# AdaLN columns and sums of output weights moved to earlier stages of an encoder block, gate transposes and a first pooling moved later

## The chip, the cores and the metric

One core of one Trainium2 chip runs the kernel. The metric is the device time of one execution in microseconds (us). TensorE (PE) multiplies matrices; VectorE (DVE), ScalarE (ACT) and GpSimd (POOL) do the rest, and SyncE (SP) issues most of the DMAs.

## What is computed

The reference is one encoder block, with B = 1, S = 2048 tokens, D = 1024, 4 mLSTM heads of 128, 4 pooling groups of 128 channels with windows 2, 4, 8 and 16, and a feed-forward width of 4096, all in float32:

```python
mod = silu(c) @ w_ada + b_ada
sh1, sc1, gt1, sh2, sc2, gt2 = split(mod, 6)
h = rmsnorm(x, g_mix) * (1 + sc1) + sh1
q, k, v, o, gates, u = split(h @ w_in, cuts)
hm = mlstm_scan(q, k, v, gates) + flip(mlstm_scan(flipped q, k, v, gates))
y_a = sigmoid(o) * rmsnorm_per_head(hm) * g_head
y_b = concat([(centred_mean(u_g, window_g) - u_g) @ w_pool[g] for g in groups]) * pool_scale
x = x + gt1 * (concat([y_a, y_b]) @ w_out)
h = rmsnorm(x, g_ffn) * (1 + sc2) + sh2
x = x + gt2 * (relu(h @ w_ff1) ** 2 @ w_ff2)
return rmsnorm(x, g_final)
```

## The kernel before

Every float32 operand of a large product is split into a high and a low part, and a product is three matmuls: high by high, low by high, high by low. For a weight, `wr` is the loaded tile (512 KB), `wh` its high part (a cast on ACT, line 395) and `wl` the low part (a subtraction on DVE, line 396). `Hh` and `Hl` are the parts of the normalised input, four blocks b of 512 tokens. `col_mm` multiplies one block by one column tile of a weight in 24 matmuls: `c15` to `c12` are the inputs u of pooling groups 3 to 0, `c4` to `c7` the heads' k and `c0` to `c3` their q.

The first 640 us consist of these stages. In the *v stage* (line 255 on) 16 token tiles of 128 run through 48 matmuls each, giving v and the gate columns; `vg_out` copies them and stores them to `vd`. In the *pooling stage* (line 415 on) groups g = 3, 2, 1, 0 each run four blocks of `col_mm(12 + g)`. After each block one step of the generator `gate_rows` (line 310) is taken: it makes the gates' running sums and maxima on DVE and ACT and transposes them on TensorE (`gT`, `gL`, `gM`, `gC`, `gD`). After block 1 the next weight is requested. After the last block of a group DVE makes the window sums s of u (lines 447 to 456), stores them to `yd`, and folds the group's output weight (`wor` scaled, a matmul `wof`, a copy `woe`, a store to `wod`). Then follow the ada columns of `MODS[g]` in `mod_col`: a load of 512 KB, a product with the activated c with its sum taken along (line 117), and an addition of the bias. Columns 16 to 23 make gt1.

After `qk_proj(0)`, which makes k and q of head 0, `scan` runs once for each head, 16 chunks of 128 tokens in both directions, with the next head's projections as filling. From head 1 on in the code, and in fact over the scans of heads 0 and 1, the generator `out_sums` (line 666) is stepped beside it: for four row tiles k it loads two rows of output weights (`os0_k` from the input, `os1_k` from `wod`), multiplies both by gt1, and stores to `wotd` three halves and four differences of halves, for the seven products of a Strassen-like output stage. Each head ends with transposes `hT` (line 632).

One pool tag, `raw`, gives all tiles `xs`, `ada`, `wr`, `wor` and `os` the same three buffers in turn. Outside the output and feed-forward stages, which are ordered by hand, a scheduler fixes the order of each engine's instructions ahead of the run; an instruction in `keep_in_program_order` is held in the order of the code. Each engine, and SP with its DMAs, then works through its list in that order. An instruction that waits holds up all that stand behind it on its engine.

## Time and profile before

| | us |
|---|---|
| median of three runs (lowest, highest) | 2042.19 (2037.84, 2043.9) |
| the profiled execution: device time | 2039.14 |
| its span in the trace | 2037.1 |
| TensorE busy, of the span | 1987.5 (98%) |
| VectorE busy | 1356.5 (67%) |
| ScalarE busy | 918.3 (45%) |

Times inside the profile count from the start of the span. A busy TensorE is not one at its peak, since matmuls overlap: a 512 column matmul is drawn with 0.39 us, but follows its forerunner by some 0.23 us. A wait is read from the bracket at the end of a timeline row: the idle time ahead of the instruction and what ended it. A granted clock (PEclk) of 1.00 is 2.4 GHz, 0.50 is 1.2 GHz.

### The profile page before, as it was taken

How to read it: one execution, taken by the hardware profiler on the slowest of the kernel's cores; microseconds unless marked ns; L12 is line 12 of the kernel's file. 1: busy time of each engine (PE TensorE's matmuls, PEld its weight loads, DVE VectorE, ACT ScalarE, POOL GpSimd, SP SyncE). 2: the span in 40 equal slices, each digit the busy share in tenths (PEclk: the TensorE clock that was granted, in tenths of full speed). 3: DMA queues.
4: the chain of work that ended last, by engine and by line, in shares of the span. 5: the costliest groups of instructions: out<-in, count | busy, mean ns of one | idle time of the engine just before them, and what ended most of it. 6: DMA issues, size and time to landing. Idle time of an engine off the chain costs nothing.

```text
span 2037.1 us, 27780 instructions
## 1 busy us (share of the span) xinstructions
PE 1987.5 (98%) x9591; PEld 1658.5 (81%) x9591; DVE 1356.5 (67%) x2456; ACT 918.3 (45%) x1704; POOL 129.7 (6%) x353
## 2 busy tenths in 40 slices
PE   7999999989999999999999999999999999999998
PEld 6997777778887888888888888888888888888886
DVE  6638636676646777555666766666877667768876
ACT  4721223333335668755556655556324224324432
POOL 1100012222210111000000000000000000000011
PEclk9999999999999999999999999999999999999999
DMA  8736867787548799765666766766887657648553
GB/s 339 237 108 209 285 205 220 253 254 226 180 131 271 236 270 315 209 196 182 224 203 224 228 226 215 226 206 225 280 268 257 225 156 262 224 158 275 187 165 132
DMA packets 298574, 452.87 MB, mean 222 GB/s; under 512 B 23569, under 2 KB 163137, under 8 KB 298306
## 3 DMA queue, kind: packets, MB, share of 16 engines
q1 hardware_dynamic: 228546, 413.35, 62.3%
q10 hardware_dynamic: 69888, 37.76, 6.1%
q8 instruction: 75, 1.23, 0.2%
q14 instruction: 65, 0.53, 0.1%
HBM read 290.40 MB, written 160.62 MB: 221 GB/s over the span
## 4 chain that ended last, share of the span: by engine, by line
PE 84%; DMA 7%; DVE 4%; issue 1%; ACT 1%; POOL 1%; SPq 1%; POOLq 0%; DVEq 0%; ACTq 0%
PE c L405 4%; PE c L404 4%; PE c L406 4%; DMA ua<-uad 1%; DMA ada<-in_w_ada 1%; DVE ada L117 1%; DMA wotd<-os 1%; DMA rob<-wotd 1%; DMA vraw<-in_w_v 1%; PE f000x L845 1%; PE o11x L845 1%; PE o10x L845 1%; PE o13x L845 1%; PE o03x L845 1%; PE o12x L845 1%
## 5 line engine op out<-in xcount | busy, mean ns | idle before, releaser
L404 PE MATMUL c<-Hh,wh 128*128 128x512 f32 x512 | 211.0, 412 | 0.0
L405 PE MATMUL c<-Hl,wh 128*128 128x512 f32 x512 | 203.4, 397 | 0.0
L406 PE MATMUL c<-Hh,wl 128*128 128x512 f32 x512 | 202.8, 396 | 0.5 <-DVE wl L396 0.5
L406 PEld LDWEIGHTS c<-Hh,wl 128*128 128x128 f32 x512 | 96.6, 189 | 20.5 <-DVE wl L396 0.9
L404 PEld LDWEIGHTS c<-Hh,wh 128*128 128x128 f32 x512 | 97.0, 189 | 17.3 <-issue 1.0
L405 PEld LDWEIGHTS c<-Hl,wh 128*128 128x128 f32 x512 | 97.1, 190 | 16.8 <-issue 0.7
L117 DVE SCALAR_TENSOR_TENSOR ada<-ada,c_bc 128x1024 f32<-128x1024 f32 x48 | 58.1, 1221 | 22.4 <-DMA ada<-in_w_ada 22.3
L581 ACT ACTIVATE ua<-ua,vcol 128x128 f32<-128x128 f32 x64 | 25.7, 401 | 103.2 <-POOL ua L577 103.1
L780 ACT CAST wb<-rwb 128x1024 fp32r<-128x1024 f32 x56 | 58.7, 1051 | 26.0 <-DMA rwb<-twd 25.8
L961 POOL TENSOR_TENSOR g300ss<-g300ss 128x1 f32<-128x1 f32 x2 | 0.9, 451 | 1079.9 <-ACT g300j L957 1079.9
L783 DVE TENSOR_TENSOR wb<-rwb,wb 128x1024 fp32r<-128x1024 f32 x56 | 68.3, 1219 | 0.8 <-ACT wb L780 0.7
L622 ACT ACTIVATE jk<-hm 128x128 bf16<-128x128 f32 x64 | 19.6, 307 | 83.0 <-DVE hm L620 82.3
L586 DVE TENSOR_TENSOR ua<-ua,q 128x256 f32<-128x256 f32 x64 | 26.4, 425 | 37.5 <-DMA ua<-uad 26.8
L577 POOL TENSOR_SCALAR_AFFINE_SELECT ua<-ua 128x128 f32<-128x128 f32 x64 | 26.6, 416 | 270.7 <-DMA ua<-uad 135.4
L625 DVE TENSOR_TENSOR hm<-hm,hss 128x256 f32<-128x256 f32 x32 | 14.7, 458 | 38.9 <-POOL hss L129 38.9
L255 PE MATMUL vgp<-vgh,Hh 128*128 128x272 f32 x128 | 38.2, 301 | 2.3 <-ACT Hh L208 2.3
L440 ACT COPY u<-c 128x512 f32<-128x512 f32 x16 | 9.4, 585 | 63.7 <-PE c L406 59.4
L783 DVE TENSOR_TENSOR ob<-rob,ob 128x1024 fp32r<-128x1024 f32 x14 | 17.1, 1224 | 30.5 <-ACT ob L780 29.9
L256 PE MATMUL v2p<-v2h,Hh 128*128 128x256 f32 x128 | 36.2, 286 | 1.1 <-ACT v2h L236 1.1
L257 PE MATMUL vgp<-vgl,Hh 128*128 128x272 f32 x128 | 37.2, 292 | 0.0
L259 PE MATMUL vgp<-vgh,Hl 128*128 128x272 f32 x128 | 37.0, 294 | 0.0
L585 DVE TENSOR_TENSOR ua<-ua,S 128x256 f32<-128x256 f32 x64 | 26.5, 413 | 14.9 <-PE S L584 14.7
(4048 smaller groups left out, 6071.3 us busy)
## 6 DMA issues: line engine op xcount, KB each, us to landing
rwb<-twd SPq DMA_DIRECT2D x56, 512.0 KB, 6.1
ada<-in_w_ada SPq DMA_DIRECT2D x48, 512.0 KB, 5.2
ua<-uad SPq DMA_DIRECT2D x64, 256.0 KB, 4.1
j<-in_w SPq DMA_DIRECT2D x32, 512.0 KB, 5.4
twd<-t SPq DMA_DIRECT2D x64, 256.0 KB, 3.0
twd<-j SPq DMA_DIRECT2D x48, 256.0 KB, 2.8
wr<-in_w_col SPq DMA_DIRECT2D x16, 512.0 KB, 4.9
q<-qkd SPq DMA_DIRECT2D x32, 256.0 KB, 3.6
```

What stands on the lines that cost most here:

```text
L117: ve.scalar_tensor_tensor(w, w, 1.0, c_bc, ALU.mult, ALU.mult, accum_out=mod[:, j:j + 1])
L255: pe.matmul(pa[:, :VG], hh, vgh[k], start=st, stop=False)
L256: pe.matmul(pb[:, :256], hh, v2h[k], start=st, stop=False)
L257: pe.matmul(pa[:, :VG], hh, vgl[k], start=False, stop=False)
L259: pe.matmul(pa[:, :VG], hl, vgh[k], start=False, stop=en)
L404: pe.matmul(ps, hh[:, k], Hh[b][:, k], start=k == 0, stop=False)
L405: pe.matmul(ps, hh[:, k], Hl[b][:, k], start=False, stop=False)
L406: pe.matmul(ps, hl[:, k], Hh[b][:, k], start=False, stop=k == KT - 1)
L577: gp.affine_select(W[:, 0], W[:, 0], pattern=[[1, P]], compare_op=ALU.is_ge, fill=NEG, base=0, channel_multiplier=-1)
L780: sc.copy(dst, src)
L783: ve.tensor_tensor(dst, src, asf(hi), ALU.subtract)
L845: pe.matmul(ps, a[:, k], b[:, k], start=start and k == 0 and n == 0, stop=k == 3 and n == 2, skip_group_check=not start)
```

## The change

Eighteen ada columns (16 to 33) move to the v stage, three after each of the tiles 8 to 13 (`VMODS`). The pooling groups keep 4 (g = 3), 6 (g = 2), 4 (g = 1) and 0 (g = 0) columns, where they had 10, 10, 8 and 4. `out_sums(k)` becomes a plain function that is called in the pooling stage, after (g, b) = (2, 2), (1, 0), (1, 2) and (0, 0), and it leaves the scans; gt1 for it comes from a transpose of columns 16 to 23 ahead of the groups. The folds of groups 3 and 2 stand behind group 3, those of 1 and 0 behind group 2. `gL` and `gC` stand one block later in the code and, like `gM`, are held there. The window sums of group 3 stand behind the first block of group 2.

```diff
@@ -28,7 +28,12 @@
 NEG = -1.0e30
 EVERY = 2
 
-MODS = (range(16, 20), range(20, 28), range(28, 38), range(38, 48))
+VMODS = {i: range(16 + 3 * (i - 8), 19 + 3 * (i - 8)) for i in range(8, 14)}
+MODS = ((), range(44, 48), range(38, 44), range(34, 38))
+
+
+FOLDS = ((), (), (1, 0), (3, 2))
+OSUMS = {(2, 2): 3, (1, 0): 2, (1, 2): 1, (0, 0): 0}
 VG = 272
 
 
@@ -298,6 +303,8 @@
                         for q in range(KT):
                             norm_later(b + 1, rb, xk, q)
                 vg_out(4 * b + j)
+                for n in VMODS.get(4 * b + j, ()):
+                    mod_col(n)
 
 
     gstack = ExitStack()
@@ -331,8 +338,9 @@
         ve.tensor_copy(lasts[fw, 1:2], m_[fw, P - 1:P])
         ve.tensor_copy(lasts[bw, 1:2], m_[bw, 0:1])
         yield
+        yield
         ps = tp("gL")
-        pe.transpose(ps[0:1, 0:P], lasts[:, 0:1], ident)
+        tc.keep_in_program_order(pe.transpose(ps[0:1, 0:P], lasts[:, 0:1], ident))
         pe.transpose(ps[0:1, P:2 * P], lasts[:, 1:2], ident)
         rows = pg.tile([1, 4, P], F32, name="g_rows")
         ve.tensor_copy(rows[:, 0:2, :], ps[0:1, 0:2 * P].rearrange("p (a n) -> p a n", a=2))
@@ -349,7 +357,7 @@
         ve.tensor_copy(r3[:, 1, :, 0:NT - 1], r2[:, 1, :, 1:NT])
         yield
         ps = tp("gM")
-        pe.transpose(ps[:, 0:1], rows[:, 3, :], ident[0:1, 0:1])
+        tc.keep_in_program_order(pe.transpose(ps[:, 0:1], rows[:, 3, :], ident[0:1, 0:1]))
         mp = gt("g_mp", 1)
         ve.tensor_copy(mp, ps[:, 0:1])
         ve.scalar_tensor_tensor(m_, b_, mp, m_, ALU.add, ALU.max)
@@ -372,8 +380,9 @@
         ve.tensor_copy(ul[fw], a[fw, P - 1:P])
         ve.tensor_copy(ul[bw], a[bw, 0:1])
         yield
+        yield
         ps = tp("gC")
-        pe.transpose(ps[:, 0:P], v, ident)
+        tc.keep_in_program_order(pe.transpose(ps[:, 0:P], v, ident))
         pe.transpose(ps[:, P:2 * P], wk, ident)
         pe.transpose(ps[:, 2 * P:3 * P], m_, ident)
         ve.tensor_copy(vcol, ps[:, 0:P])
@@ -411,6 +420,21 @@
     def mod_row(j0):
         return mod_d[j0:j0 + KT, :].rearrange("(o a) n -> o (a n)", o=1).broadcast_to([P, D])
 
+    def out_sums(k, gt1):
+
+        rows = [raw(f"os{h}_{k}") for h in range(2)]
+        for h, src in enumerate((w_o[k], wo_d[k])):
+            dma(rows[h], src)
+        for h in range(2):
+            ve.tensor_tensor(rows[h], rows[h], gt1, ALU.mult)
+        b11, b12, b21, b22 = [r[:, 512 * n:512 * n + 512] for r in rows for n in range(2)]
+        for place, b in ((0, b11), (1, b21), (5, b22)):
+            dma(wot_d[place, :, k], b)
+        for place, dst, x_, y_ in ((3, b11, b12, b11), (4, b12, b22, b12), (2, b22, b22, b11),
+                                   (6, b21, b21, b22)):
+            ve.tensor_tensor(dst, x_, y_, ALU.subtract)
+            dma(wot_d[place, :, k], dst)
+
 
     with tc.tile_pool(name="pu", bufs=2) as pu, tc.tile_pool(name="psU", bufs=2, space=PSUM) as psU:
         wpl = pu.tile([P, 4, P], F32, name="wpl", bufs=1)
@@ -420,10 +444,37 @@
         pgs = ExitStack()
         pg = pgs.enter_context(tc.tile_pool(name="pg", bufs=1))
         gates = gate_rows(pg)
-        w = col_weights(15)
-        for g in (3, 2, 1, 0):
+
+        def pooled(g, u, pinned):
+
             win = WIN[g]
             hw = win // 2
+            s = pu.tile([P, T + 16], F32, tag="s", name=f"s{g}", bufs=1)
+            n = T + 15
+            ins = ve.tensor_tensor(s[:, 0:n], u[:, 0:n], u[:, 1:n + 1], ALU.add)
+            if pinned:
+                tc.keep_in_program_order(ins)
+            d = 2
+            while d < win:
+                n -= d
+                ve.tensor_tensor(s[:, 0:n], s[:, 0:n], s[:, d:n + d], ALU.add)
+                d *= 2
+            s = s[:, 8 - hw:8 - hw + T]
+            ve.tensor_tensor(s[:, 0:8], s[:, 0:8], edgec[:, 16 * g:16 * g + 8], ALU.mult)
+            ve.tensor_tensor(s[:, T - 8:T], s[:, T - 8:T], edgec[:, 16 * g + 8:16 * g + 16], ALU.mult)
+            ve.scalar_tensor_tensor(s, s, 1.0 / win, u[:, 8:8 + T], ALU.mult, ALU.subtract)
+            for b in range(NB):
+                dma(y_d[b][:, 4 + g, :], s[:, 512 * b:512 * b + 512])
+
+        w = col_weights(15)
+        mt = tp("modT1")
+        pe.transpose(mt[0:KT, 0:P], mod[:, 16:16 + KT], ident)
+        me = evt("modT1e")
+        sc.copy(me[0:KT, 0:P], mt[0:KT, 0:P])
+        dma(mod_d[16:16 + KT, :], me[0:KT, 0:P])
+        gt1 = pu.tile([P, D], F32, name="gt1", bufs=1)
+        dma(gt1, mod_row(16))
+        for g in (3, 2, 1, 0):
             u = pu.tile([P, T + 16], F32, tag="u", name=f"u{g}")
             gp.memset(u[:, 0:8], 0.0)
             gp.memset(u[:, T + 8:T + 16], 0.0)
@@ -440,32 +491,26 @@
                 sc.copy(u[:, 8 + 512 * b:8 + 512 * b + 512], ps)
                 if b == 1:
                     wn = col_weights(11 + g if g else 4)
+                if (g, b) in OSUMS:
+                    out_sums(OSUMS[g, b], gt1)
+                if (g, b) == (2, 0):
+                    pooled(3, u3, True)
             w = wn
-
-            s = pu.tile([P, T + 16], F32, tag="s", name=f"s{g}", bufs=1)
-            n = T + 15
-            ve.tensor_tensor(s[:, 0:n], u[:, 0:n], u[:, 1:n + 1], ALU.add)
-            d = 2
-            while d < win:
-                n -= d
-                ve.tensor_tensor(s[:, 0:n], s[:, 0:n], s[:, d:n + d], ALU.add)
-                d *= 2
-            s = s[:, 8 - hw:8 - hw + T]
-            ve.tensor_tensor(s[:, 0:8], s[:, 0:8], edgec[:, 16 * g:16 * g + 8], ALU.mult)
-            ve.tensor_tensor(s[:, T - 8:T], s[:, T - 8:T], edgec[:, 16 * g + 8:16 * g + 16], ALU.mult)
-            ve.scalar_tensor_tensor(s, s, 1.0 / win, u[:, 8:8 + T], ALU.mult, ALU.subtract)
-            for b in range(NB):
-                dma(y_d[b][:, 4 + g, :], s[:, 512 * b:512 * b + 512])
-
-            wr = raw(f"wor{g}")
-            dma(wr, w_o[4 + g])
-            ve.tensor_scalar(wr, wr, pscale[:, g:g + 1], None, ALU.mult)
-            for n in range(2):
-                ps = psU.tile([P, 512], F32, tag="y", name=f"wof{g}_{n}")
-                pe.matmul(ps, wpl[:, g], wr[:, 512 * n:512 * n + 512], start=True, stop=True)
-                e = evt(f"woe{g}_{n}")[:, :512]
-                sc.copy(e, ps)
-                dma(wo_d[g][:, 512 * n:512 * n + 512], e)
+            if g == 3:
+                u3 = u
+            else:
+                pooled(g, u, False)
+
+            for f in FOLDS[g]:
+                wr = raw(f"wor{f}")
+                dma(wr, w_o[4 + f])
+                ve.tensor_scalar(wr, wr, pscale[:, f:f + 1], None, ALU.mult)
+                for n in range(2):
+                    ps = psU.tile([P, 512], F32, tag="y", name=f"wof{f}_{n}")
+                    pe.matmul(ps, wpl[:, f], wr[:, 512 * n:512 * n + 512], start=True, stop=True)
+                    e = evt(f"woe{f}_{n}")[:, :512]
+                    sc.copy(e, ps)
+                    dma(wo_d[f][:, 512 * n:512 * n + 512], e)
             for j in MODS[g]:
                 mod_col(j)
         pgs.close()
@@ -663,26 +708,6 @@
                 sc.copy(e, ps)
                 dma_act(o_d[b][:, h, :], e)
 
-        def out_sums(gt1):
-
-            for k in range(4):
-                rows = [raw(f"os{h}_{k}") for h in range(2)]
-                for h, src in enumerate((w_o[k], wo_d[k])):
-                    dma(rows[h], src)
-                yield
-                for h in range(2):
-                    ve.tensor_tensor(rows[h], rows[h], gt1, ALU.mult)
-                    yield
-                b11, b12, b21, b22 = [r[:, 512 * n:512 * n + 512] for r in rows for n in range(2)]
-                for place, b in ((0, b11), (1, b21), (5, b22)):
-                    dma(wot_d[place, :, k], b)
-                yield
-                for place, dst, x_, y_ in ((3, b11, b12, b11), (4, b12, b22, b12), (2, b22, b22, b11),
-                                           (6, b21, b21, b22)):
-                    ve.tensor_tensor(dst, x_, y_, ALU.subtract)
-                    yield
-                    dma(wot_d[place, :, k], dst)
-
         def chain(*gs):
             for g in gs:
                 yield from g
@@ -695,9 +720,6 @@
         me = evt("modTe")
         sc.copy(me[0:48, 0:P], mt[0:48, 0:P])
         dma(mod_d, me[0:48, 0:P])
-        gt1 = wp.tile([P, D], F32, tag="bc", name="gt1", bufs=1)
-        dma(gt1, mod_row(16))
-        osum = out_sums(gt1)
         for h in range(H):
             Cn = [None] * NT
             if h + 1 < H:
@@ -709,8 +731,6 @@
                 n += 1
                 if n % EVERY == 0:
                     next(fill, None)
-                if h > 0 and n % 4 == 0:
-                    next(osum, None)
             for _ in fill:
                 pass
             Cb = Cn
```

What this does to the engines' order is shown at three places. The names: `vd3` is the store of block 3's v, `vt13` the tile it is from, `xs15` a token tile of x.

SP at the end of v, before:

```order
L189 DMA xs15_1045<-in_x 128x1024
L392 DMA wr15_1577<-in_w_col 128x1024
L392 DMA wr14_1661<-in_w_col 128x1024
L271 DMA vd2_129<-vt8_1158 128x4x129
L461 DMA wor3_1766<-in_w_o 128x1024
```

SP in the last tiles of v, in the changed kernel:

```order
L276 DMA vd3_130<-vt13_1498 128x4x129
L126 DMA ada31_1503<-in_w_ada 128x1024
L126 DMA ada32_1507<-in_w_ada 128x1024
L126 DMA ada33_1511<-in_w_ada 128x1024
L401 DMA wr15_1649<-in_w_col 128x1024
L276 DMA vd3_130<-vt14_1566 128x4x129
L401 DMA wr14_1740<-in_w_col 128x1024
```

The load of c15's weight, `wr15`, stood behind the last token tile, some six tiles of v ahead of its use; it stands behind `ada33` and the store of tile 13's v now.

VectorE at the low part of c12's weight, before; s1 are group 1's window sums, `u1` its input:

```order
L396 TENSOR_TENSOR wl12_2066<-wr12_2063,wh12_2065 128x1024
L462 TENSOR_SCALAR wor1_2131<-wor1_2131,pscale_241 128x1024
L447 TENSOR_TENSOR s1_2121<-u1_2008 128x2063
L117 SCALAR_TENSOR_TENSOR ada20_2144,mod_90<-ada20_2144,c_bc_87 128x1024
L451 TENSOR_TENSOR s1_2121<-s1_2121 128x2061
```

VectorE at the same place in the changed kernel; `os0_2` and `os1_2` are the two rows of `out_sums(2)`:

```order
L122 SCALAR_TENSOR_TENSOR ada43_2086,mod_90<-ada43_2086,c_bc_87 128x1024
L454 TENSOR_TENSOR s1_2237<-u1_2090 128x2063
L128 TENSOR_TENSOR mod_90<-mod_90,bada_200 128x1
L429 TENSOR_TENSOR os0_2_2119<-os0_2_2119,gt1_1660 128x1024
L429 TENSOR_TENSOR os1_2_2120<-os1_2_2120,gt1_1660 128x1024
L460 TENSOR_TENSOR s1_2237<-s1_2237 128x2061
L435 TENSOR_TENSOR os0_2_2119<-os0_2_2119 128x512
L405 TENSOR_TENSOR wl12_2165<-wr12_2162,wh12_2164 128x1024
```

`wl12` stood ahead of the first sum over u1; it stands behind two sums, two products with gt1 and one subtraction now.

VectorE at the low part of c4's weight, before; s0 and `u0` belong to group 0:

```order
L117 SCALAR_TENSOR_TENSOR ada27_2172,mod_90<-ada27_2172,c_bc_87 128x1024
L123 TENSOR_TENSOR mod_90<-mod_90,bada_200 128x1
L396 TENSOR_TENSOR wl4_2234<-wr4_2231,wh4_2233 128x1024
L462 TENSOR_SCALAR wor0_2298<-wor0_2298,pscale_241 128x1024
L117 SCALAR_TENSOR_TENSOR ada16_2311,mod_90<-ada16_2311,c_bc_87 128x1024
L447 TENSOR_TENSOR s0_2289<-u0_2176 128x2063
```

VectorE at the same place in the changed kernel:

```order
L454 TENSOR_TENSOR s0_2393<-u0_2263 128x2063
L128 TENSOR_TENSOR mod_90<-mod_90,bada_200 128x1
L122 SCALAR_TENSOR_TENSOR ada47_2259,mod_90<-ada47_2259,c_bc_87 128x1024
L429 TENSOR_TENSOR os0_0_2292<-os0_0_2292,gt1_1660 128x1024
L128 TENSOR_TENSOR mod_90<-mod_90,bada_200 128x1
L429 TENSOR_TENSOR os1_0_2293<-os1_0_2293,gt1_1660 128x1024
L463 TENSOR_TENSOR s0_2393<-s0_2393,edgec_1644 128x8
L464 TENSOR_TENSOR s0_2393<-s0_2393,edgec_1644 128x8
L465 SCALAR_TENSOR_TENSOR s0_2393<-s0_2393,u0_2263 128x2048
L435 TENSOR_TENSOR os0_0_2292<-os0_0_2292 128x512
L405 TENSOR_TENSOR wl4_2338<-wr4_2335,wh4_2337 128x1024
```

`wl4` stood ahead of the first sum over u0; it stands behind all of s0, one ada column and the products of `out_sums(0)` now.

## Rows read from the trace of the kernel before

**Rows 1.** Part 4 of the page: shares of the chain that ended last.

```profile
PE 84%; DMA 7%; DVE 4%; issue 1%; ACT 1%; POOL 1%; SPq 1%; POOLq 0%; DVEq 0%; ACTq 0%
```

**Rows 2.** Waits of PE: line, waited for; us in total, times, longest.

```profile
PE gL L335 <- issue: 4.1, 1, 4.1
...
PE kvb L508 <- DMA wr<-in_w_col: 1.0, 1, 1.0
```

**Rows 3.** Windows: stretch; us busy (and count) per engine, PEclk, DMA share, GB/s.

```profile
110.00:120.00 10.00, 10.00 (x85) 10.00 (x85) 1.08 (x4) 0.75 (x2) 0.10 (x1) 1.00 0.19 54
155.60:159.00 3.40, 3.36 (x10) 2.67 (x10) 3.37 (x13) 0.00 (x0) 0.00 (x0) 0.50 0.27 54
```

**Rows 4.** Timeline of PE at gL: start us, us, instruction [idle before <-releaser].

```profile
155.34 0.27 PE L335 MATMUL gL<-ident,g_last 128*1 128x128 f32 x1 [4.06 <-issue]
```

**Rows 5.** Groups of instructions, 134 to 256 us: busy us, mean ns | idle before.

```profile
L117 DVE SCALAR_TENSOR_TENSOR ada<-ada,c_bc 128x1024 f32<-128x1024 f32 x32 | 38.9, 1221 | 16.8 <-DMA ada<-in_w_ada 16.7
...
L447 DVE TENSOR_TENSOR s<-u 128x2063 f32<-128x2063 f32 x4 | 9.2, 2303 | 0.2 <-ACT u L440 0.2
L456 DVE SCALAR_TENSOR_TENSOR s<-s,u 128x2048 f32<-128x2048 f32 x4 | 9.1, 2286 | 0.0
...
L396 DVE TENSOR_TENSOR wl<-wr,wh 128x1024 fp32r<-128x1024 f32 x5 | 6.1, 1224 | 5.9 <-ACT wh L395 5.9
L395 ACT CAST wh<-wr 128x1024 fp32r<-128x1024 f32 x5 | 5.3, 1051 | 13.0 <-DMA wr<-in_w_col 11.2 <-PE v2p L260 1.9
```

**Rows 6.** The tile os: ns min/median/max, first and last start.

```profile
L674 DVE TENSOR_TENSOR os<-os,gt x8: 1212/1226/1226, 302.6 to 436.1; 128x1024 f32<-128x1024 f32 x8
L682 DVE TENSOR_TENSOR os<-os x8: 681/691/692, 307.6 to 446.0; 128x512 f32<-128x512 f32 x8
```

**Rows 7.** DMA issues, 134 to 256 us: KB each, median us to landing.

```profile
ada<-in_w_ada SPq DMA_DIRECT2D x32, 512.0 KB, 4.3
...
wr<-in_w_col SPq DMA_DIRECT2D x6, 512.0 KB, 4.7
```

**Rows 8.** Timeline of DVE in the last tiles of v.

```profile
123.12 0.42 DVE L269 COPY vt<-v2p 128x256 f32<-128x256 f32 x1
...
132.77 1.23 DVE L396 TENSOR_TENSOR wl<-wr,wh 128x1024 fp32r<-128x1024 f32 x1 [3.41 <-ACT wh L395]
```

**Rows 9.** Timelines of ACT and then of PE at c12.

```profile
211.15 0.59 ACT L440 COPY u<-c 128x512 f32<-128x512 f32 x1 [0.41 <-PE c L406]
...
212.05 0.50 PE L406 MATMUL c<-Hh,wl 128*128 128x512 f32 x1 [0.47 <-DVE wl L396]
212.71 1.13 PE L465 MATMUL wof<-wor,wpl 128*128 128x512 f32 x2 [0.17 <-DVE wor L462]
```

**Rows 10.** Timeline of PE at the first c4 matmuls.

```profile
235.73 0.39 PE L404 MATMUL c<-Hh,wh 128*128 128x512 f32 x1
235.95 0.39 PE L405 MATMUL c<-Hl,wh 128*128 128x512 f32 x1
237.12 1.98 PE L465 MATMUL wof<-wor,wpl 128*128 128x512 f32 x4 [0.78 <-DVE wor L462]
```

**Rows 11.** Timeline of PE: first and last hT of heads 0 and 2, last of head 1.

```profile
308.11 0.27 PE L632 MATMUL hT<-ident,hm 128*128 128x128 f32 x1
...
372.13 0.30 PE L632 MATMUL hT<-ident,hm 128*128 128x128 f32 x1 [0.84 <-DVE hm L625]
...
454.11 0.30 PE L632 MATMUL hT<-ident,hm 128*128 128x128 f32 x1 [0.96 <-DVE hm L625]
...
471.17 0.27 PE L632 MATMUL hT<-ident,hm 128*128 128x128 f32 x1
...
529.42 0.30 PE L632 MATMUL hT<-ident,hm 128*128 128x128 f32 x1 [0.85 <-DVE hm L625]
```

**Rows 12.** Timelines of DVE and of PE in the scan of head 1.

```profile
394.84 1.23 DVE L674 TENSOR_TENSOR os<-os,gt 128x1024 f32<-128x1024 f32 x1 [1.28 <-DMA os<-in_w_o]
...
396.38 0.49 PE L597 MATMUL n<-Cf,ua 128*128 128x129 f32 x2 [1.47 <-DVE Cf L607]
```

## The prediction

> **What bounds the kernel now.** I read the page first, then the waits of TensorE, then the stretches in which it waits, instruction by instruction. The chain of work that ended last is TensorE for 84% of the span [rows 1], so only what TensorE waits for is worth anything. From the output stage on (about 640 us to the end) it hardly waits, and the change does not reach there. It acts on four stretches of the first 460 us: the last tiles of v, the pooling stage (134 to 236 us), the first block of k, and the scans of heads 0 and 1. In the pooling stage the largest wait is gL, 4.1 us [rows 2]; after it the granted clock is 0.50 for 3.4 us, the 1.2 GHz level [rows 3, 4]. The waits at c12 and at wof0 are 0.5 and 0.8 us [rows 9, 10]. In the middle of v, VectorE has work for 1.08 of 10 us [rows 3]. In the scans VectorE holds TensorE up whenever an out_sums operation stands before the carried state Cf: at 394.84 it waits 1.28 us for os, works 1.23 us, and TensorE loses 1.47 us [rows 12].
>
> The sum is made against the profiled execution, 2039.14 us (span 2037.1). The median of the three runs, 2042.19, is 3.05 us above it; I take the difference as it comes out and put it on the median.
>
> **The change, part by part.**
>
> *v stage.* Eighteen ada columns cost VectorE 18 x 1.22 = 22 us [rows 5]; between tiles 8 and 15 it has that time, and TensorE does not wait for the columns. So the operations cost nothing while v lasts. Their loads are the price: SP issues wr15 only behind ada33, and its buffer is freed by ada31's product. Tile 13's copies end at about 123.5 [rows 8]; its store is issued, then ada31's load, at 123.9. Loads take 4.3 (ada) and 4.7 us (wr) in this stretch [rows 7]: ada31 at 128.2, its product 129.5, wr15 at 134.2, the cast of 1.05 and the subtraction of 1.22 us [rows 5] at 136.5. TensorE wants wl15 at 134.9, and in the kernel before it was done at 134.0 [rows 8]. **Cost +1.6** (0 to 3).
>
> The Trainium skill, page "DMA: Bandwidth & Descriptors", section on the anatomy of one DMA, fits 2.0 us plus the bytes over 436 GB/s, on another issue path than SP's; for 512 KB an estimate of 3.2 us. The rows are longer, 4.3 and 4.7. By the page's price wr15 would come 2.6 us earlier and the sum of all terms would be about 3 us lower, since c4 below also hangs on loads in a row.
>
> *Gate transposes.* gL stands after the whole of group 3 (near 158 us) instead of inside it. Its input was ready at 155.3 [rows 4], VectorE has fewer ada columns in front, so the wait of 4.1 and the half-clock stretch after it (3.4 us at half rate, 1.7 lost [rows 3]) both go: **-5.8**. What is late next is wof1, ahead of c13: its weight's scaling stands on VectorE behind the whole of group 3's pooling, which now begins after c14_0 (about 167.6). That is five wide operations of 2.2 to 2.3 us, three subtractions of 0.6, the small gate work and the scaling, some 17.5 us, while TensorE has 16.4 us of matmuls. **+1.3** (0 to 3); the other gate transposes have a block each and wait for nothing new.
>
> *c12, the last group's weights.* Before, wl12 was computed ahead of group 1's pooling and TensorE waited 0.47 us for it, and 0.17 for wof1 [rows 9]. Now it stands on VectorE behind the first add of s1, two products with gt1, the second add and one subtraction. The first add needs the whole of u1, that is the copy of c13's last block, and TensorE has nothing left then but four matmuls of c12 (0.9 us at 0.23 each [rows 10]). From the copy's start: 0.59 + 2.2 + 1.2 + 1.2 + 2.2 + 0.6 + 1.2 = 9.2 us [rows 5, 6, 9], with start-up 9.4, less 0.9: **+8.5**, less the 0.6 of before. This is a floor of the written order; loads can only lengthen it (wr12 waits for ada43's product, whose load waits behind the stores of s2). Range 7.9 to 11.
>
> *c4, the first k weights.* The same again: wl4 stands behind the first add of s0 (it needs c12's last block), ada47's product, two products with gt1, the edge products, the final step of s0 and one subtraction: 0.6 + 2.2 + 1.3 + 2.4 + 0.3 + 2.2 + 0.6 + 1.2 = 10.8, less four matmuls: floor 9.9. Here loads come close as well: ada44 to ada47 are issued behind the stores of out_sums(1), then the two rows of out_sums(0) and wr4 each behind a product, three loads of 4.3 to 4.7 us in a row. I take **+11** (9.6 to 14), nearer to the floor since only one of the chains has to be late for more; less the 0.8 of wof0's wait, which goes [rows 10].
>
> *The clock.* The waits at c12 and c4 are both longer than the one that was followed by 3.4 us at 0.50 [rows 3, 4], so each is charged **+1.7** (0 to 1.8).
>
> *out_sums leaves the scans.* Eight products of 1.23 and sixteen subtractions of 0.69, eight of which are in the row [rows 6], are 21 us of VectorE; what counts is the length of a head. From the last hT of head 0 to that of head 1 is 82.0 us, from there to that of head 2, which has no such work, 75.3: **-6.7**. Within head 0 the hT span 64.0 us, within head 2 58.25: **-5.8** [rows 11]. Together -12.5 (10 to 14; the heads have the same matmuls, but head 0's start is not aligned).
>
> *First block of k.* kvb waited 1.0 us [rows 2]; with TensorE 18 us later the loads there have landed: **-1** (-2.5 to +1).
>
> Sum: 1.6 - 5.8 + 1.3 + (8.5 - 0.6 + 1.7) + (11 - 0.8 + 1.7) = +18.6 up to k; -12.5 - 1 after it: **+5.1 us**. The profiled execution would take 2044.2, the median 2047.
>
> **The rivals.**
>
> *Faster: the moved work meets idle engines.* If wl15 and wof1 come in time, both waits are at their floors and no clock falls, the stage costs -5.8 + (7.9 - 0.6) + (9.6 - 0.8) = +10.3; with the best of the scans and of k (-14, -2.5) the change gains 6.2 us: 2036. For it: VectorE is idle in v and held TensorE up in the scans [rows 3, 12]. Against it: the floors follow from the order of one engine, and a wait of 4.1 us did lower the clock. The Trainium skill, page "Perfetto Trace Analysis", section Optimization Strategy, says that a kernel whose most contended engine changes over time may gain by interleaving these stretches; by that rule the change ends here. No run shows it yet. Chance 0.12, of which 0.11 lies beyond the bound named below.
>
> *Slower: the SP queue decides.* SP issues in program order, and now 28 stores and 8 loads of out_sums stand there among the ada loads. If ada47's load lands after about 247 us (some 5 us instead of 4.3 for each of the three before it), wr4 is issued later than VectorE's own chain allows, c4 waits 14 instead of 11; the same at c12 makes 11 out of 8.5, and wof1 3 out of 1.3. That is +3 + 2.5 + 1.7 = +7.2 on the forecast, +12.3 in all: 2054.5. For it: landings in the tuned stretch are already 4.3 to 4.7 [rows 7], and the stage gains traffic. A seventh of this price already passes the upper bound. Chance 0.37.
>
> *The change doesn't do what it says.* gL's input could be late even after c15_3, if the four ada columns of group 3 hold VectorE as before; then 2 to 4 us of the 5.8 come back: 2050. The transposes have 11 us more than before, so this has 0.04, counted among the slower ones.
>
> **How the numbers follow.** A measurement here can tell 0.3%, 6.1 us, from no change: below 2036.1 is faster, above 2048.3 slower. The forecast of 2047 lies inside, close to the upper bound; it has the rest, 0.47, and the terms' ranges around it (about 4 us either way, taken as independent) put 0.03 of this above the bound. So faster is 0.11; same 0.44 and the 0.01 of the gainful rival that stays inside, 0.45; slower 0.37, 0.04 and 0.03, 0.44. The forecast's own range is 2043 to 2051; the range that should hold the time 8 times in 10 reaches to most of both rivals, 2039 to 2057.
>
> **What would show it.** In the profile of the changed kernel: no wait at gL and a granted clock of 1.00 from 150 to 160 us; a wait of TensorE for wl of 8 us or more at c12 (near 212 us) and of 10 or more at c4 (near 245), each with matmuls at half rate behind it; no os operations after 302 us, and the last hT of heads 0, 1 and 2 some 75 us apart. If the waits at c12 and c4 are a few us only, the order on VectorE is not what binds there and the kernel is faster; if the heads stay 82 us apart, something other than out_sums sets their length and it is slower by far.

## The result and the profile after

The changed kernel takes 2053.0 us (median of four runs, 2051.45 to 2054.18) and the kernel before 2041.79 beside it: a ratio of 1.0060, 95% interval 1.0047 to 1.0073. It is slower by 0.6%, some 12 us. The two profiled executions, 2054.17 and 2039.14, lie 15.0 us apart, at spans of 2052.4 and 2037.1; the traces are compared on that pair, and about 3 us of their distance are a matter of which executions were profiled.

In the changed kernel TensorE is busy for 1991.9 us, 97% of the span. The shares of the chain that ended last ([rows 1] of before):

```profile
PE 86%; DMA 6%; DVE 5%; ACT 1%; issue 1%; POOL 0%; SPq 0%; DVEq 0%; POOLq 0%; ACTq 0%
```

The largest waits of TensorE in the changed kernel, with total, times and longest in us ([rows 2] of before):

```profile
PE c L413 <- ACT wh L404: 22.0, 3, 10.1
```

The wait for gL is gone. In its place stand three waits for the high part of a weight, `wh`, which is cast once the tile has landed, one for a scaled output weight, `wor`, and one for a low part, `wl`. The timeline of TensorE shows where: c15, wof1, c12 (twice) and c4.

```profile
142.93 0.79 PE L413 MATMUL c<-Hh,wh 128*128 128x512 f32 x1 [6.68 <-ACT wh L404]
...
198.08 2.93 PE L510 MATMUL wof<-wor,wpl 128*128 128x512 f32 x3 [3.73 <-DVE wor L507]
...
230.17 0.79 PE L413 MATMUL c<-Hh,wh 128*128 128x512 f32 x1 [5.22 <-ACT wh L404]
...
234.32 0.80 PE L415 MATMUL c<-Hh,wl 128*128 128x512 f32 x1 [2.08 <-DVE wl L405]
...
267.64 0.79 PE L413 MATMUL c<-Hh,wh 128*128 128x512 f32 x1 [10.06 <-ACT wh L404]
```

The four stretches behind these waits, in the view of [rows 3]:

```profile
142.93:146.30 3.37, 3.33 (x7) 2.22 (x8) 2.92 (x5) 1.46 (x3) 0.00 (x0) 0.50 0.91 293
...
198.00:201.40 3.40, 3.32 (x5) 1.51 (x5) 1.38 (x4) 0.58 (x1) 0.00 (x0) 0.53 1.04 382
...
230.00:238.70 8.70, 6.45 (x14) 4.67 (x15) 8.43 (x10) 0.12 (x1) 0.00 (x0) 0.50 0.69 207
267.60:272.80 5.20, 5.05 (x11) 3.56 (x12) 4.15 (x6) 0.00 (x0) 0.00 (x0) 0.50 0.80 299
```

The matmuls there are drawn with 0.63 instead of 0.39 us, the granted clock is 1.2 GHz. At half rate 3.33, 3.32, 6.45 and 5.05 us of work lost about 1.7, 1.6, 3.2 and 2.5 us.

The transposes hT, as in [rows 11]: the first of head 0, then the last of heads 0, 1 and 2.

```profile
336.57 0.27 PE L677 MATMUL hT<-ident,hm 128*128 128x128 f32 x1
...
394.65 0.30 PE L677 MATMUL hT<-ident,hm 128*128 128x128 f32 x1 [0.85 <-DVE hm L670]
...
470.37 0.30 PE L677 MATMUL hT<-ident,hm 128*128 128x128 f32 x1 [0.91 <-DVE hm L670]
...
544.35 0.30 PE L677 MATMUL hT<-ident,hm 128*128 128x128 f32 x1 [0.85 <-DVE hm L670]
```

The scans start 28.5 us later than before (336.57 against 308.11) and give 13.5 us back: head 0 spans 58.1 us instead of 64.0, head 1 75.7 instead of 82.0, head 2 74.0 instead of 75.3. After them nothing changes: the last matmul starts 15.2 us later than before.

**Why c15 waits.** VectorE, then SP, then ACT at the end of v:

```profile
127.93 1.23 DVE L122 SCALAR_TENSOR_TENSOR ada<-ada,c_bc 128x1024 f32<-128x1024 f32 x1 [1.57 <-DMA ada<-in_w_ada]
...
129.38 0.42 DVE L274 COPY vt<-v2p 128x256 f32<-128x256 f32 x1
...
135.93 1.23 DVE L122 SCALAR_TENSOR_TENSOR ada<-ada,c_bc 128x1024 f32<-128x1024 f32 x1 [3.46 <-DMA ada<-in_w_ada]
...
130.07 0.38 SPq L276 DMA_DIRECT2D vd<-vt  x1
130.50 2.14 SPq L126 DMA_DIRECT2D ada<-in_w_ada  x3
137.20 0.33 SPq L401 DMA_DIRECT2D wr<-in_w_col  x1
...
141.83 1.04 ACT L404 CAST wh<-wr 128x1024 fp32r<-128x1024 f32 x1 [4.02 <-DMA wr<-in_w_col]
```

The last matmul of tile 13 starts at 123.89, but VectorE works in order and waits for an ada load until 127.93; only after that product is the copy of the tile's v made, at 129.38. SP holds the store of that copy ahead of the next three ada loads, so they go out at 130.50. wr15 waits for the product of the first of them, which waits for its load until 135.93, and is issued at 137.20; TensorE has no weight until 142.93. VectorE waits for an ada load, and SP behind it for VectorE's copy. In the last four tiles with columns the longest of VectorE's waits were 1.8, 3.4, 1.6 and 3.5 us.

**Why c4 and c12 wait.** VectorE, SP and ACT ahead of c4:

```profile
253.16 1.23 DVE L122 SCALAR_TENSOR_TENSOR ada<-ada,c_bc 128x1024 f32<-128x1024 f32 x1 [1.60 <-DMA ada<-in_w_ada]
...
257.20 1.23 DVE L122 SCALAR_TENSOR_TENSOR ada<-ada,c_bc 128x1024 f32<-128x1024 f32 x1 [2.62 <-DMA ada<-in_w_ada]
...
259.69 2.30 DVE L454 TENSOR_TENSOR s<-u 128x2063 f32<-128x2063 f32 x1
...
261.98 1.22 DVE L122 SCALAR_TENSOR_TENSOR ada<-ada,c_bc 128x1024 f32<-128x1024 f32 x1
...
268.55 1.22 DVE L405 TENSOR_TENSOR wl<-wr,wh 128x1024 fp32r<-128x1024 f32 x1
...
263.23 0.33 SPq L401 DMA_DIRECT2D wr<-in_w_col  x1
...
266.54 1.04 ACT L404 CAST wh<-wr 128x1024 fp32r<-128x1024 f32 x1 [8.35 <-DMA wr<-in_w_col]
```

wr4 takes the buffer that ada47's product (261.98) sets free. That product stands behind three others, two of which wait for their loads (1.60 and 2.62 us), and behind the first add of s0 (259.69). TensorE ends c12 at 257.6 and stands until 267.64. c12 has the same form: ada41 to ada43 keep the three raw buffers, the first of their products waits 5.7 us for its load, and wr12 is issued only at 224.47; its cast starts at 229.08.

The loads are one half of it. The other half is VectorE's list, shown here at c12 (ACT's copy of the last block of u1 first):

```profile
224.99 0.58 ACT L491 COPY u<-c 128x512 f32<-128x512 f32 x1 [4.85 <-PE c L415]
...
225.67 2.31 DVE L454 TENSOR_TENSOR s<-u 128x2063 f32<-128x2063 f32 x1 [1.23 <-issue]
...
233.05 1.22 DVE L405 TENSOR_TENSOR wl<-wr,wh 128x1024 fp32r<-128x1024 f32 x1
```

From the first add of s1 to the end of wl12, 234.27, VectorE works without a gap. TensorE gets wh12 at 230.17, runs the four matmuls that need no wl, and waits again, until 234.32. At c4 wl4 ends at 269.77 and TensorE goes on with it at 269.82. So with this order on VectorE an earlier wr12 or wr4 alone would have gained next to nothing (an estimate from these rows).

### The profile page after: what moved, and what is told of

It is laid out like the page before. It is cut to its first block, busy times and chain, and to the rows that moved or that the text cites. A ratio compares the mean times of both kernels' runs of the same rounds, so it can differ in the third digit from the quotient of the medians.

```text
span 2052.4 us, 27805 instructions
## 1 busy us (share of the span) xinstructions
PE 1991.9 (97%) x9592; PEld 1663.4 (81%) x9592; DVE 1363.1 (66%) x2456; ACT 919.7 (45%) x1705; POOL 128.0 (6%) x353
## 4 chain that ended last, share of the span: by engine, by line
PE 86%; DMA 6%; DVE 5%; ACT 1%; issue 1%; POOL 0%; SPq 0%; DVEq 0%; POOLq 0%; ACTq 0%
PE c L415 5%; PE c L414 5%; PE c L413 5%; DMA ada<-in_w_ada 2%; DVE ada L122 1%; PE S L629 1%; PE n L640 1%; PE kvf L647 1%; PE n L643 1%; DVE xk L224 1%; PE n L645 1%; PE n L642 1%; DMA vraw<-in_w_v 1%; DMA ua<-uad 1%; PE f000x L865 1%
```

## The experiments

Two readings were to be told apart. By the first, each wait is the price of one moved part and goes with it. By the second, the waits hang together through the raw buffers and SP's list, so that a wait taken away at one place comes back at the next. The diffs are against the changed kernel unless said otherwise; where one shows only lines with a +, these take the place of the changed kernel's.

**The sums back in the scans.**

```diff
-                if (g, b) in OSUMS:
-                    out_sums(OSUMS[g, b], gt1)
...
+                if h > 0 and n % 4 == 0:
+                    next(osum, None)
```

> The changed kernel with out_sums back in the scans (columns in v, folds, gates and the late first pooling stay). Theory A, waits for weights: in the changed kernel the loss sits in four waits of TensorE, for c15's weight (6.9 us), for wof1's scaled weight (3.7), for c12's (5.4 + 2.2) and for c4's (10.2), because the loads of ada columns, output rows and weights take turns in three buffers and one queue; without out_sums there, the last three go (under 1 us each) and the scans of heads 0 and 1 get their 12.5 us back: against the kernel before +1.6 for the end of v, +8.6 for c15's wait with its half-clock stretch, -5.8 for gL, -1 for waits of before that go: +3 us (0 to 6). Theory B, amount of work: the stage is full of VectorE work and traffic, whatever their order; then the columns alone cost as well, two of the three waits stay in part, and it is +10 or more against before. Last hT of heads 0 and 1: 82 us apart by both.

Measured 2035.5 us, ratio 0.9971 (0.9960 to 0.9981): faster than before, where a loss of 3 was expected. The wait at c15 stays (5.4 us), those at wof1, c12 and c4 go, and the first k transposes come at 249.1 us, 3 later than before and 29 earlier than in the changed kernel. The forecast held up to there; then the way from there to the last hT of head 3 took 6.5 us less than before, 3.9 of them up to the first hT, which the sum didn't hold. Moving the sums into the pooling stage thus costs 0.9%, 18 us, net of the 12 that the scans gain.

**Fifteen columns in v instead of eighteen**, the other three in group 3.

```diff
-VMODS = {i: range(16 + 3 * (i - 8), 19 + 3 * (i - 8)) for i in range(8, 14)}
-MODS = ((), range(44, 48), range(38, 44), range(34, 38))
+VMODS = {i: range(16 + 3 * (i - 8), 19 + 3 * (i - 8)) for i in range(8, 13)}
+MODS = ((), range(44, 48), range(38, 44), range(31, 38))
```

> The changed kernel with the three columns of tile 13 (31 to 33) taken back to group 3. Theory A: the load of c15's weight stands behind one turn less of the three buffers; the wait of 6.9 us at the start of the pooling stage falls to under 1.5 and its half-clock stretch (1.7) goes, while the other waits stay: 7 us (5 to 9) less than the changed kernel, so +4 against before. Theory B: three more columns in the pooling stage cost what they save, it stays at +11 (+8 to +13).

Measured 2055.54, 1.0077 (1.0062 to 1.0092): no gain. TensorE's timeline at c12 and c4:

```profile
229.88 0.79 PE L413 MATMUL c<-Hh,wh 128*128 128x512 f32 x1 [11.81 <-ACT wh L404]
...
265.58 0.80 PE L413 MATMUL c<-Hh,wh 128*128 128x512 f32 x1 [11.85 <-ACT wh L404]
```

The wait at c15 fell from 6.7 to 1.4 us, as expected, but c12 starts at 229.88 instead of 230.17 and only waits longer for it. The loads and products ahead of wr12 set that time, and what is saved ahead of them is worth nothing: the second reading.

**Only the gate transposes**, on the kernel before; the third transpose, gC, likewise.

```diff
         yield
+        yield
         ps = tp("gL")
-        pe.transpose(ps[0:1, 0:P], lasts[:, 0:1], ident)
+        tc.keep_in_program_order(pe.transpose(ps[0:1, 0:P], lasts[:, 0:1], ident))
...
-        pe.transpose(ps[:, 0:1], rows[:, 3, :], ident[0:1, 0:1])
+        tc.keep_in_program_order(pe.transpose(ps[:, 0:1], rows[:, 3, :], ident[0:1, 0:1]))
```

> The kernel before with the later gate transposes alone (gL and gC one block later, the three held in their places); columns, out_sums, folds and first pooling as before. Theory A: the wait of 4.1 us at gL and the 1.7 us of its half-clock stretch go and nothing takes their place: -5.8 us (-7 to -4). Rival: group 3's window sums stand on VectorE between gL and gM, so the wait moves to gM or gC and at most 2 us are gained.

Measured 2039.93, 1.0001 (0.9991 to 1.0011). TensorE first, then VectorE:

```profile
171.46 0.23 PE L353 MATMUL gM<-ident,g_rows 1*128 1x1 f32 x1 [3.99 <-DVE g_rows L350]
...
168.84 2.27 DVE L453 TENSOR_TENSOR s<-s 128x2061 f32<-128x2061 f32 x1
171.04 0.17 DVE L349 COPY g_rows<-g_rows 1x60 f32<-1x60 f32 x1
```

The 4.1 us of gL come back as 4.0 us at gM, whose input stands behind group 3's window sums on VectorE.

**The sums in the scans, without the two further `yield`s** (against the first experiment; the same ahead of gC).

```diff
         yield
-        yield
         ps = tp("gL")
```

> The kernel with the sums in the scans (18 columns in v), but gL and gC stand where they stood before. If the later transposes matter once the columns of group 3 are fewer, gL waits 3 to 4 us with a half-clock stretch: 4 to 6 us more than with them, about 0 against before. If four columns instead of ten ahead of the gates are enough by themselves, gL finds its input and the kernel stays at -5 against before.

Measured 2041.71, 1.0001 (0.9992 to 1.0010), against 0.9971 with them. gL waits 1.3 us and a fold 1.4:

```profile
162.27 0.27 PE L342 MATMUL gL<-ident,g_last 128*1 128x128 f32 x1 [1.34 <-issue]
```

The kernel with the columns in v gains nothing without the later transposes, the transposes alone gain nothing, both together 0.3%. The reading that VectorE must be free of ada columns *and* gL must stand where its input is ready fits this, but it isn't shown: the two kernels with the columns also have the moved folds and the first pooling put off, and the folds were never tested by themselves. The two waits are 2.8 of these 6 us; the rest isn't traced.

**The first pooling not put off.**

```diff
-                if (g, b) == (2, 0):
-                    pooled(3, u3, True)
...
-            if g == 3:
-                u3 = u
-            else:
-                pooled(g, u, False)
+            pooled(g, u, False)
```

> The changed kernel with the first pooling back behind group 3; all else stays. Theory A2 (a weight's arrival at c12 is fixed by the chain of loads and products ahead of it, so a wait saved earlier is only useful if this chain also moves): s3 and with it the stores, the columns and wr12 behind it come about 9 us earlier; wof1's wait of 3.7 us goes, c12's of 7.6 falls to 2 to 5, gM may take a new wait of up to 4 as in the kernel with the gates alone; 5 us less than the changed kernel (2 to 9), so +6 against before. Rival (TensorE's waits add up, each by itself): only wof1's wait goes and gM's comes, +11.

Measured 2046.7, 1.0023 (1.0011 to 1.0034), some 7 us better than the changed kernel. wof1 and c12 wait 0.9 and 2.4 us, but c4 15 instead of 10:

```profile
261.35 0.80 PE L413 MATMUL c<-Hh,wh 128*128 128x512 f32 x1 [14.88 <-ACT wh L404]
```

The pooling put off behind the transposes thus costs some 7 of the 12 us of loss in this kernel; the other 5 have another cause, and what went at c12 came back in part at c4: the second reading again.

**Ten columns (38 to 47) behind the last group**, so that no ada load of theirs stands ahead of wr12 and wr4.

```diff
-MODS = ((), range(44, 48), range(38, 44), range(34, 38))
+MODS = (range(38, 48), (), (), range(34, 38))
```

> The changed kernel with the ten columns 38 to 47 behind group 0 instead of behind groups 2 and 1; out_sums, folds, gates and the columns in v stay. Theory A: it is the turn in the three buffers (c12's weight behind ada43's product, c4's behind ada47's) that makes these weights late; with the columns out of the way both waits (7.6 and 10.2 us) fall to under 2 us each and their half-clock stretches go, so 18 us (14 to 21) less than the changed kernel, of which the ten columns beside the first k blocks give back up to 4: -5 against before (-8 to 0). Theory B: out_sums itself fills the stage; the waits at c12 and c4 keep over half of their length and the kernel stays slower than before.

Measured 2048.9, 1.0044 (1.0029 to 1.0058). VectorE at c12, and then TensorE and SP in the first k block:

```profile
220.89 1.23 DVE L405 TENSOR_TENSOR wl<-wr,wh 128x1024 fp32r<-128x1024 f32 x1 [2.66 <-ACT wh L404]
222.54 2.31 DVE L454 TENSOR_TENSOR s<-u 128x2063 f32<-128x2063 f32 x1 [0.43 <-ACT u L491]
...
277.09 0.77 PE L553 MATMUL kvb<-va,kb 128*128 128x129 f32 x2 [8.98 <-DMA v<-vd]
...
255.94 12.07 SPq L126 DMA_DIRECT2D ada<-in_w_ada  x7
...
272.68 0.83 SPq L608 DMA_DIRECT2D v<-vd  x1
```

The waits at c12 and c4 are gone (0.2 and 0.5 us), with all the sums still in the pooling stage, and wl12 stands *ahead* of s1 again, though only columns were moved. That the scheduler goes by the time at which the load can come is the likely reason; it isn't shown. But SP now needs 12 us for seven ada loads ahead of the next weight and of the loads of v, and TensorE waits 9 us for those. The loss moved one stage on: 8 us over before, where 5 under it were expected.

**The sums beside the first q projection**, with fifteen columns in v, and before it, to separate the two, **the sums in the scans with fifteen columns** (the first two experiments' edits together). The first one's edit, beside the fifteen columns:

```diff
-        for _ in qk_proj(0, Cb):
-            pass
+        for n, _ in enumerate(qk_proj(0, Cb)):
+            if n in (8, 13, 18, 23):
+                out_sums((n - 8) // 5, gt1)
```

> As the kernel with 15 columns and the sums in the scans, but out_sums is called beside the k and q projections of head 0, after its 9th, 14th, 19th and 24th step. If the scans of heads 0 and 1 are long because of out_sums, their last hT come 75 instead of 81 us apart and 12 us more are gained: -22 against before (-26 to -14). Rival, from the kernel with the late columns: loads and stores ahead of va in SP's order make kvb wait, 4 to 9 us go back: -13 or worse. If the heads stay 81 us apart, something else sets them.

> The kernel with the sums in the scans, and 15 columns in v instead of 18 (31 to 33 in group 3). Theory A2: here no late weight follows that would swallow it, so the fall of c15's wait from 5.4 to some 1.5 us and its half-clock stretch (1.7) reach the end: 5 us less than the kernel with the sums in the scans, which was 0.29% under before, so -10 against before (-12 to -7). Rival: a wait at c14, c13 or c12 takes it up as at c12 with the sums in the pooling stage, -5 as without this edit.

Measured 2040.8, 0.9999 (0.9990 to 1.0007), and 2036.11, 0.9972 (0.9962 to 0.9983). Beside q, the last hT of heads 0, 1 and 2 are some 75 us apart, as wanted, but the first scan starves. TensorE there, and in the kernel before at the same place:

```profile
270.00:310.00 40.00, 31.35 (x138) 25.79 (x137) 20.02 (x45) 8.75 (x19) 3.92 (x10) 0.86 0.90 305
```

```profile
268.00:308.00 40.00, 39.31 (x204) 32.79 (x203) 14.94 (x40) 7.54 (x20) 4.68 (x8) 1.00 0.54 174
```

TensorE is busy for 31.4 of these 40 us instead of 39.3, at a clock of 0.86: 16 of the 28 stores and 3 of the 8 loads of the sums are issued in this stretch, among the scan's own loads. Whether their place in SP's list holds the scan up or the traffic itself (DMA share 0.90 instead of 0.54), no run separates. In the other kernel c15 still waits 3.8 us, for wl15 behind a scaling of wor that waits 6.1 us for its load, and a new wait of 2.1 us appears at wof0, so that three columns fewer in v bring nothing there either.

**Columns 38 to 47 one at a time inside the first q projection**, the sums in the pooling stage.

> The kernel with the late columns, but its ten columns 38 to 47 are requested one by one, beside every second step of head 0's k and q projections, instead of in one go behind group 0. With them in one go c12 and c4 no longer waited, and TensorE waited 9 us at kvb instead, for va behind ten loads in SP's queue. Theory (each load costs where it stands ahead of a needed one in the queue): c12 and c4 go on not waiting, the wait at kvb falls from 9 to under 3 us, heads 0 and 1 stay 75 us long: 9 us (6 to 13) less than with the late columns, which was 8 over before, so -1 against before (-5 to +2). Rival: the ten loads meet the first loads of scan 0 as the sums did beside the first q; scan 0 starts 5 to 10 us late, and it stays at +5 or more.

Measured 2038.82, 0.9991 (0.9981 to 1.0001), as expected: with the sums still in the pooling stage, the loss is gone. c12 and c4 wait 0.2 and 0.4 us, c15 waits 5.5, and the start of the first scan 3.4:

```profile
300.47 0.80 PE L626 MATMUL S<-q 128*128 128x128 f32 x2 [3.35 <-DVE ua L627]
```

**The same with twelve columns in v.**

```diff
+VMODS = {i: range(16 + 3 * (i - 8), 19 + 3 * (i - 8)) for i in range(8, 12)}
+MODS = (range(31, 34), range(28, 31), (), range(34, 38))
```

> The changed kernel with its sums left in the pooling stage, but twelve columns in v (28 to 30 in group 1 of the gates, 31 to 33 in group 0, 34 to 37 in group 3) and the last ten, 38 to 47, asked for one at a time inside the first q projection, with the sums' second half after them. Theory: c15's wait (5.7 us and some 1.7 us of clock in the run with 15 columns) goes, and with it most of the loss; the heads stay about 75 apart; 2033 us (ratio 0.996), between 0.994 and 0.999. Rival: the wait comes back as c12's or c4's, because the sums' loads and stores now stand ahead of them, and the time stays within 2 us of 2039.

Measured 2036.7, 0.9983 (0.9971 to 0.9994). The wait at c15 is gone, but c4 waits 6.5 us, since wr4's buffer again depends on an ada product that waits for its load. VectorE, then TensorE:

```profile
234.45 1.23 DVE L122 SCALAR_TENSOR_TENSOR ada<-ada,c_bc 128x1024 f32<-128x1024 f32 x1 [5.51 <-DMA ada<-in_w_ada]
...
240.88 0.79 PE L413 MATMUL c<-Hh,wh 128*128 128x512 f32 x1 [6.51 <-ACT wh L404]
```

The wait came back where the rival had it, at c4, and less than half of the gain of 0.4% that was expected is left, though the ratio lies inside the theory's range. This trace is of a run that took 2032.11.

**Twelve columns in v and the sums in the scans** as in the first experiment, first with six columns behind group 2, then with three of them behind group 3 instead.

```diff
+VMODS = {i: range(16 + 3 * (i - 8), 19 + 3 * (i - 8)) for i in range(8, 12)}
+MODS = (range(31, 34), (28, 29, 30, 44, 45, 46, 47), range(38, 44), range(34, 38))
```

```diff
+MODS = (range(31, 34), (28, 29, 30, 44, 45, 46, 47), range(41, 44), range(34, 41))
```

> The kernel with the sums in the scans, and 12 columns in v (tiles 8 to 11; 28 to 30 go to group 1, 31 to 33 to group 0). With 18 columns c15's weight came 5.5 us late, with 15 still 4.7 and a fold waited 2.3 us for its weight. With 12 its load stands behind the columns of tile 11 and ahead of tile 12's v store: no wait over 1 us at c15, no half-clock stretch, folds as with 18: 6 us (3 to 8) less than with 18, which was 5 under before, so -11 (-13 to -8). Rival: the wait moves on to wof as with 15, or the columns moved to groups 1 and 0 make c12 or c4 wait: -5 as before.

> The kernel with twelve columns in v and the sums in the scans (0.9959), with columns 38 to 40 handed from group 2 of the gates to group 3, so that c12's raw block can be cast three columns earlier. Theory: what was left of c12's wait there, 4.2 us for a cast that stood behind a product of u, goes; the time falls to about 12 us below the kernel before (2029, ratio 0.994). Rival: the three columns lengthen VectorE's queue in group 3 and the wait turns up as wof0's, 2 us and a stretch at half clock, as it did where columns were taken out of v with six more in group 3; then nothing is gained against 0.9959.

Measured 2032.98, 0.9959 (0.9945 to 0.9972), and 2031.0, 0.9955 (0.9938 to 0.9971). Both beat both kernels; between them the intervals show no difference. c15 no longer waits in either. What is left, ACT and TensorE of the first (the trace of a run that took 2038.27), then TensorE of the second:

```profile
228.64 1.05 ACT L404 CAST wh<-wr 128x1024 fp32r<-128x1024 f32 x1 [12.74 <-DMA wr<-in_w_col]
...
230.22 0.50 PE L413 MATMUL c<-Hh,wh 128*128 128x512 f32 x1 [4.07 <-ACT u L468]
```

```profile
189.78 3.37 PE L485 MATMUL wof<-wor,wpl 128*128 128x512 f32 x4 [3.15 <-DVE wor L482]
```

The expectation of the second had the first row the wrong way round: the cast doesn't stand behind the work on u, it stands *ahead* of two copies of u on ACT and holds them up while wr12 is on its way. With three columns fewer ahead of wr12 that wait goes, and a fold, queued behind group 3's window sums on VectorE, waits 3.15 us instead.

## Why the prediction was right, and where it was wrong

The forecast was 2047 and no measurable change. 2053.0 lies in the range of 2039 to 2057, but above the forecast's own 2043 to 2051, and by the bound of 0.3% that the prediction set itself the change is slower, to which it gave a chance of 0.44, against 0.45 for no change. The number is nearest to the rival in which SP's queue decides (2054.5). Term by term, in us of the profiled pair, the half clock counted with its wait:

| step | forecast | trace |
|---|---|---|
| c15 at the end of v | +1.6 | +8.4 (6.7 + 1.7) |
| gL | -5.8 | -5.8 |
| wof1 | +1.3 | +5.2 (3.7 + 1.6, less 0.17 of before) |
| c12 | +9.6 | +9.9 (5.2 + 2.1 + 3.2, less 0.6) |
| c4 | +11.9 | +11.8 (10.1 + 2.5, less 0.8) |
| first k transposes | +18.6 | +31.9 |
| first k block | -1 | -3.4 |
| heads 0 and 1 | -12.5 | -12.2 (5.9 + 6.3) |
| head 2 and the rest | 0 | -1.1 |
| sum | +5.1 | +15.2 |

The five terms make 29.5 of the 31.9 us; v itself ended 1.6 us later, and 0.8 are spread over small gaps that weren't followed.

**Right:** the scans, to 0.3 us. In all six kernels with the sums in the pooling stage, head 0 spans 58.1 to 58.6 us and the last hT of head 1 follows 74.7 to 75.7 behind head 0's; in all seven with the sums in the scans (the kernel before among them) it is 62.4 to 65.4 and 80.0 to 82.0. So the difference read off [rows 11] is the sums' own price. gL went as said, with its stretch at half clock; with the transposes alone its wait came back at gM, which no rival of the prediction had named. c12 and c4 came out within 0.3 us of their terms.

**The step that failed most is the v stage.** "Tile 13's copies end at about 123.5" was read from a trace in which VectorE had little else to do there [rows 3, 8]. The prediction said itself that SP issues ada31 behind that store, but let the copy keep its old time; in the changed kernel it stands behind a product that waits for a load, and is made at 129.38. That the operations "cost nothing while v lasts" nearly held for TensorE (v ended 1.6 us later), but not for the copies and the stores behind them. This term is 6.8 of the 10.1 us by which the sum was short. With twelve columns in v the wait doesn't occur.

**wof1**, the second step: s3's sums were to begin at about 167.6, behind c14_0. VectorE in the changed kernel:

```profile
175.40 1.23 DVE L405 TENSOR_TENSOR wl<-wr,wh 128x1024 fp32r<-128x1024 f32 x1 [4.35 <-ACT wh L404]
...
178.74 1.23 DVE L429 TENSOR_TENSOR os<-os,gt 128x1024 f32<-128x1024 f32 x1 [2.11 <-DMA os<-in_w_o]
...
183.47 2.31 DVE L454 TENSOR_TENSOR s<-u 128x2063 f32<-128x2063 f32 x1
...
197.27 0.75 DVE L507 TENSOR_SCALAR wor<-wor,pscale 128x1024 f32<-128x1024 f32 x1
```

They begin at 183.47, behind wl13, which waits for its weight until 175.40, and behind both products of `out_sums(3)`, the first of which waits for its row until 178.74. The 16 us of delay were partly covered by TensorE being late itself.

**c12 and c4: size and mechanism as forecast, but not alone.** The prediction derived them from the written order on VectorE, with loads as something that "can only lengthen" a floor. At c12 that chain took 9.3 us from the start of u1's copy to the end of wl12, where the sum had 9.4; at c4 it took 12.2 (257.61 to 269.77) where the floor had 10.8, since s0's first add stood behind an ada product that had waited for loads. The waits that the trace names first, though, are for `wh`, a load: the loads were late as well, by less than the chain at c12 and by about as much at c4. The clock was mis-sized: 1.7 us were charged behind each wait, 3.2 and 2.5 came; at c12 some of that fell into VectorE's chain and made the waits shorter than the forecast 8.5. The order itself, which the prediction took as given, wasn't: where ten columns were moved away, wl12 stood ahead of s1 again and both waits fell to 0.5 us or less with the sums still there. No run had the early load without the better order, or the other way round. Nor do the terms add: with 15 columns in v, 5.3 us less wait at c15 gave nothing, since c12's start stayed at 230.

**The rivals.** Interleaving (2036) didn't come: the moved work met idle engines, but not an idle queue. The Trainium skill, page "Perfetto Trace Analysis", section Optimization Strategy, says that interleaving stretches whose most contended engine differs may improve a kernel. Here it did for columns in v together with later transposes (0.9955 to 0.9972) and did not for the sums, which at every place tried did worse than in the scans: 1.0060 in the pooling stage, 0.9983 and 0.9991 there with the columns moved out of the way, 0.9999 beside q. The rival on SP's queue had nearly the right total, in part by luck: the excess over the forecast was found at c15 and wof1, 10.7 us, and not at c12 and c4, where it had put 5.5 of its 7.2. Of its loads, ada took a median of 4.7 us from issue to landing between 126 and 290 us (4.3 before, [rows 7]). The estimate of 3.2 us by the Trainium skill, page "DMA: Bandwidth & Descriptors", section on the anatomy of one DMA, is not borne out for this queue in this stretch.

The heads in the experiments with the sums put elsewhere, some 75 us apart, show that the gain of 12 us is there to be had; every place found for the sums took more than that: compared with the sums in the scans and as many columns in v, the kernels are 0.2 to 1.1% slower.

## What to carry to other kernels

Before work is moved to a stage where an engine idles, list its loads and stores in the issuing queue and ask which load that TensorE needs next will stand behind them, and in whose buffer it must land. An engine that works in order and waits there for a load holds up also the old, small instructions behind it, so no time of the old trace may be kept for these. A wait that is set by the arrival of a load is not shortened by anything that ends earlier ahead of it. And where a wait has two causes that end at nearly the same time, here a load and the list of an engine, the one that the trace names is not enough to go by: look for what ends just behind it.

## What was not expected of the hardware

The length of a wait alone doesn't tell whether the clock falls behind it. After waits of 2.7 us (for wof1) and 2.4 us (at the first scan), both in the kernel with spread columns and twelve in v, the granted clock stayed at 1.00; after 2.2 us at the first kvb, with twelve columns and the sums in the scans, it was 0.53 in the next 3.4 us:

```profile
187.70:191.00 3.30, 3.30 (x9) 1.33 (x9) 1.41 (x3) 1.46 (x3) 0.00 (x0) 1.00 1.04 382
...
296.40:299.80 3.40, 3.29 (x23) 2.90 (x24) 2.44 (x6) 3.01 (x6) 0.00 (x0) 1.00 0.44 166
```

```profile
254.30:257.70 3.40, 3.40 (x11) 2.83 (x12) 0.65 (x2) 0.00 (x0) 0.00 (x0) 0.53 0.95 265
```

Behind each wait of 3.7 us and more that is shown above, the clock of the next 3.4 us was 0.50 to 0.55; behind those at c12 and c4 it stayed at 0.50 for 6.45 and 5.05 us of work. What decides between these cases was left open; in a sum, each wait of 2 to 3 us should carry 0 to 1.7 us for the clock, and a longer one, or two close together, up to 3.2.
